# A third plane, -sin, in the rotation table of an S5 scan inside a two-block fp32 kernel

## The chip, the cores and the metric

The kernel runs on one core of one Trainium2 chip. The metric is device time in microseconds (us), median of several runs. A profiled execution of the kernel gives the rows shown below; their times count from the start of that execution's span. Engines are named as the profile names them: PE (matmuls) and PEld (its weight loads), DVE (VectorE), ACT (ScalarE), POOL (GpSimd), SP (SyncE, which here only issues DMAs).

## The reference, cut to what matters

Two blocks in sequence, all in fp32. Block 1 has two layers of four kinds of attention (differential, windowed, neighbourhood, query/key-normalised), each with an input projection, heads and an output projection. Block 2 has an input projection, a latent attention, a state-space branch (S5), a gated unit and a convolutional feed-forward network. Only the S5 branch computes what the change touches. For each of 32 groups of 128 complex states it runs, over the 272 time steps held (the last 258 are used),

```
x[t] = lambda * x[t-1] + B u[t]          (complex, one lambda per state)
y[t] = Re(C x[t]) + D u[t],   then a tanh-gelu
```

The kernel writes lambda as r * exp(i*theta) and rotates: with m[t] = exp(-i*theta*t) * (B u)[t], the scan g[t] = r * g[t-1] + m[t] has a real factor, so the real and the imaginary part are two separate real scans, and x[t] = exp(i*theta*t) * g[t]. The table of cos(theta*t) and sin(theta*t) for one group n is 2 planes of 128 x 272 values.

## The kernel before

**Weights.** All large matmuls are fp32 done as three passes over split operands: a weight tile of 128x1024 is loaded by SP into `raw` (3 buffers), ACT casts its high part `wh` (L314, 4 buffers), DVE subtracts to get the low part `wl` (L328), and PE runs 24 matmuls on the tile: data high x wh (L468), data low x wh (L469), data high x wl (L470). The method `take` asks for `wl` of the tile at hand and for `wh` of up to three tiles after it, so ACT's casts are issued, in program order, ahead of PE's use.

**Side work.** Other work is written as Python generators that are advanced a step at each `yield`, a few steps per weight tile, so its instructions stand between those of the tiles on each engine's queue. Every engine runs its queue strictly in the order of the program.

**The table.** `s5_tables` is such side work. It runs beside block 1's second layer, from about 1377 to 1777 us: first the input projection and heads (to about 1720 us), then the output projection (the "out phase", weight tiles 280 to 311, which ends at about 1771 us). For each n = 0..31 it copies 32 columns into a tile `et` (ACT, L1056), doubles the table in four levels, four DVE instructions each (L1068 to L1071; the last level is 16 wide, so the row `L1071 ... 128x16` is the last piece of an n), and stores the tile to the DRAM table `etab` by a DMA that POOL issues (L1072). `et` has two buffers. The 2 KB tiles that `t2k` hands out (`ea`, `eb`, `tb`, `bo`, the output phase's `sq`, the gate's `gt`) share a ring of three buffers with the tag `t2`.

**The out phase.** For every pair of output rows ACT copies the sums (`hb`, L1489) and squares them (`sq`, L1494), and POOL adds the squares up (`acc`, L1496). At its end PE sums over partitions (L577), POOL raises to -1/2 (`rr`, L584), PE transposes `rr`, and block 2 starts.

**The use.** `s5()` runs beside block 2's input projection and heads, from about 1827 to 2082 us. SP loads `e` (one n of `etab`, 2 buffers); `rotate` (L1812) makes two products on DVE, each over both planes (L1817), two sums of 272 (L1818, L1819), two scans (L1822), and on POOL two products of 516 (L1825) and two sums of 258 (L1826, L1827).

Of the kernel before, what the change touches and what calls it, by code (L numbers as in the profile page):

```python
# [11 lines left out]
F32 = mybir.dt.float32  # L12
F32R = mybir.dt.float32r
I32 = mybir.dt.int32
AF = mybir.ActivationFunctionType
ALU = mybir.AluOpType
AX = mybir.AxisListType
ADD, SUB, MUL, MAX = ALU.add, ALU.subtract, ALU.mult, ALU.max
# [79 lines left out]
NT = 272  # L98
NQ = 258
# [146 lines left out]
def program(ctx: ExitStack, tc: tile.TileContext, A, stop=None):  # L246
    nc = tc.nc
    V, S, P, T, SY = nc.vector, nc.scalar, nc.gpsimd, nc.tensor, nc.sync
# [4 lines left out]
    dram = ctx.enter_context(tc.tile_pool(name="dram", bufs=1, space=bass.MemoryType.DRAM))  # L253
# [286 lines left out]
    gpo = const.tile([128, 2, 16], F32, name="gpo")  # L540
    s5r = const.tile([128, 32], F32, name="s5r")
    acc272 = const.tile([128, NT], F32, name="acc272")
    etab = dram.tile([32, 128, 2, NT], F32, name="etab")

    btab = dram.tile([2, 32, 32, 2, 128], F32, name="btab")
    half = cst("half", [128, 2], "half")
# [67 lines left out]
    def t2k(name="t2"):  # L614
        return aw.tile([128, 512], F32, tag="t2", name=name, bufs=3)
# [295 lines left out]
    def s5_tables():  # L911
# [83 lines left out]
        for i in range(2):  # L995
            n0 = 16 * i
            b = aw.tile([128, 2, NT], F32, tag="mraw", name="bri", bufs=2).rearrange("p v t -> p (v t)")[:, :512]
            SY.dma_start(out=b, in_=A["bri"][:, n0:n0 + 16].rearrange("p n v c -> p (n v c)"))
            b = b.rearrange("p (n v c) -> p n v c", v=2, c=16)
            yield  # L1000
            yield
            fr, fi = (s5f[:, v, n0:n0 + 16].unsqueeze(2).to_broadcast([128, 16, 16]) for v in range(2))
            for v, op in enumerate((SUB, ADD)):
                tab = t2k("tb").rearrange("p (a n c) -> p a n c", a=2, c=16)
                V.tensor_tensor(out=tab[:, 0], in0=b[:, :, v, :], in1=fr, op=MUL)
                V.tensor_tensor(out=tab[:, 1], in0=b[:, :, 1 - v, :], in1=fi, op=MUL)
                V.tensor_tensor(out=tab[:, 0], in0=tab[:, 0], in1=tab[:, 1], op=op)
                o = t2k("bo").rearrange("p (n g c) -> p n g c", g=2, c=16)
                for g_ in range(2):
                    S.activation(out=o[:, :, g_, :], in_=tab[:, 0], func=AF.Copy, scale=half[:, g_:g_ + 1])  # L1010
                yield
                yield from hold()
                pt, of = ps_("X"), o.rearrange("p n g c -> p (n g c)")
                for q in range(4):
                    T.transpose(pt[:, 128 * q:128 * q + 128], of[:, 128 * q:128 * q + 128], ident)
                yield
                hl = [aw.tile([128, 512], F32R, tag="t2", name="bhl", bufs=3) for _ in range(2)]
                split(hl[0], hl[1], pt)
                lock["X"] = False
                for b_, t in zip(range(2), hl):  # L1020
                    P.dma_start(out=btab[b_, n0:n0 + 16, :, v, :].rearrange("(q a) c p -> (a c) q p", a=4), in_=t.bitcast(F32).rearrange("p (q s) -> p q s", q=4))
# [14 lines left out]
        for n in range(32):  # L1036
            e = aw.tile([128, 2, NT], F32, tag="mraw", name="et", bufs=2)
            if n % 8 == 0:
                V.memset(e0[:, :, 0, 0:1], 1.0)
                V.memset(e0[:, :, 1, 0:1], 0.0)  # L1040
                for lev in range(5):
                    if lev > 1:
                        yield
                        yield
                    tab = t2k("ea").rearrange("p (v n t) -> p v n t", v=2, n=8)
                    L = 1 << lev
                    c, s_ = (pw[:, lev, v, n:n + 8].unsqueeze(2).to_broadcast([128, 8, L]) for v in range(2))
                    xr, xi, er, ei = (e0[:, :, v, i * L:i * L + L] for i in range(2) for v in range(2))
                    ta, tb = tab[:, 0, :, :L], tab[:, 1, :, :L]
                    V.tensor_tensor(out=ta, in0=xi, in1=s_, op=MUL)  # L1050
                    V.tensor_tensor(out=tb, in0=xi, in1=c, op=MUL)
                    V.tensor_tensor(out=er, in0=xr, in1=c, op=MUL)
                    V.tensor_tensor(out=ei, in0=xr, in1=s_, op=MUL)
                    V.tensor_tensor(out=er, in0=er, in1=ta, op=SUB)
                    V.tensor_tensor(out=ei, in0=ei, in1=tb, op=ADD)
            S.copy(out=e[:, :, 0:32], in_=e0[:, n % 8])  # L1056
            for lev in range(5, 9):
                if lev < 8 and (lev != 6 or n % 2):
                    yield
                    yield  # L1060
                if lev < 8:
                    tab = t2k("eb").rearrange("p (v t) -> p v t", v=2)
                L = 1 << lev
                w = min(L, NT - L)
                c, s_ = pw[:, lev, 0, n:n + 1], pw[:, lev, 1, n:n + 1]
                er, ei = e[:, 0, L:L + w], e[:, 1, L:L + w]
                ta, tb = tab[:, 0, :w], tab[:, 1, :w]
                V.tensor_scalar(ta, e[:, 1, :w], s_, None, op0=MUL)  # L1068
                V.tensor_scalar(tb, e[:, 1, :w], c, None, op0=MUL)
                V.scalar_tensor_tensor(out=er, in0=e[:, 0, :w], scalar=c, in1=ta, op0=MUL, op1=SUB)  # L1070
                V.scalar_tensor_tensor(out=ei, in0=e[:, 0, :w], scalar=s_, in1=tb, op0=MUL, op1=ADD)  # L1071
            P.dma_start(out=etab[n], in_=e)  # L1072


    have, done_o = {}, {}
# [572 lines left out]
    def ring(tag, n, bufs):  # L1648
        return mw.tile([128, n], F32, tag=tag, name=tag, bufs=bufs)

    def chunks(t, off, n, w):
        return [t[:, off + i * w:off + i * w + w] for i in range(n)]
# [3 lines left out]
    ZF = zb(F32)  # L1656
# [131 lines left out]
    def s5():  # L1788
# [8 lines left out]
        def load_e(n):  # L1797
            c = mw.tile([128, 2, 32], F32, tag="ct", name="ct", bufs=7)
            SY.dma_start(out=c, in_=A["ct"][n])
            e = mw.tile([128, 2, NT], F32, tag="e", name="e", bufs=2)  # L1800
            SY.dma_start(out=e, in_=etab[n])
            return e, c

# [6 lines left out]
            return t  # L1810

        def rotate(n, bu, e):  # L1812
            co, si = e[:, 0, :], e[:, 1, :]
            m = ring("a1", 2 * NT, 1).rearrange("p (v t) -> p v t", v=2)
            g = ring("a2", 2 * NT, 2).rearrange("p (v t) -> p v t", v=2)
            for o, b in ((m, bu[0]), (g, bu[1])):
                V.tensor_tensor(out=o, in0=b[:, :NT].unsqueeze(1).to_broadcast([128, 2, NT]), in1=e, op=MUL)  # L1817
            V.tensor_tensor(out=m[:, 0, :], in0=m[:, 0, :], in1=g[:, 1, :], op=ADD)  # L1818
            V.tensor_tensor(out=m[:, 1, :], in0=m[:, 1, :], in1=g[:, 0, :], op=SUB)  # L1819
            rr = s5r[:, n:n + 1].to_broadcast([128, NT])  # L1820
            for v in range(2):
                V.tensor_tensor_scan(g[:, v, :], rr, m[:, v, :], 0.0, op0=MUL, op1=ADD)  # L1822
            o, o_ = (ring(t, 2 * NQ, k).rearrange("p (v t) -> p v t", v=2) for t, k in (("pr0", 5), ("pr", 1)))
            for x, w in ((o, co), (o_, si)):
                P.tensor_tensor(out=x, in0=g[:, :, 14:], in1=w[:, 14:].unsqueeze(1).to_broadcast([128, 2, NQ]), op=MUL)  # L1825
            P.tensor_tensor(out=o[:, 0, :], in0=o[:, 0, :], in1=o_[:, 1, :], op=ADD)  # L1826
            P.tensor_tensor(out=o[:, 1, :], in0=o[:, 1, :], in1=o_[:, 0, :], op=SUB)  # L1827
            out = [o[:, v, :] for v in range(2)]
            return out

        todo = deque()

        def gelu(j, yps):
            y, w = ring("gy", NQ, 1), ring("gw", NQ, 1)

            def a():
                V.scalar_tensor_tensor(out=y, in0=uF(j), scalar=dsk[:, j:j + 1], in1=yps[:, :NQ], op0=MUL, op1=ADD)
                S.activation(out=w, in_=y, func=AF.Square, scale=math.sqrt(0.044715))

            def b():  # L1840
                V.scalar_tensor_tensor(out=w, in0=w, scalar=1.0, in1=y, op0=ADD, op1=MUL)
                S.activation(out=w, in_=w, func=AF.Tanh, scale=math.sqrt(2 / math.pi))

            def c():
                V.scalar_tensor_tensor(out=w, in0=w, scalar=1.0, in1=y, op0=ADD, op1=MUL)
                S.activation(out=gF(j), in_=w, func=AF.Copy, scale=0.5)
                S.activation(out=uu[0][j][:, :NQ], in_=w, func=AF.Copy, scale=0.5)

            def d():
                V.tensor_tensor(out=uu[1][j][:, :NQ], in0=gF(j), in1=uu[0][j][:, :NQ].bitcast(F32), op=SUB)  # L1850

            todo.extend((a, b, c, d))
# [494 lines left out]
```

## Time and profile before

| what | value |
|---|---|
| median of 3 runs | 2967.01 us (2963.41 to 2968.47) |
| the profiled execution's own time | 2966.05 us |
| its span | 2964.0 us |
| PE busy | 2779.8 us, 94% |
| DVE busy | 1932.1 us, 65% |
| ACT busy | 1252.2 us, 42% |
| POOL busy | 489.5 us, 17% |

The span is what the profile's rows cover; the execution's own time is 2.05 us more. PE is busy for almost all of the span, and the other engines for a half or less on average. These averages cover stages that differ, so the rows below are taken from the stretches that the change touches.

### The profile page before, as it was taken

The page shows a single profiled execution, that of the slowest core. Times are in us where ns is not written, and L with a number is a line of the kernel's source. Part 1 is how long each engine was busy: PE and PEld are TensorE (multiplying, and loading weights), DVE is VectorE, ACT ScalarE, POOL GpSimd, SP SyncE. Part 2 cuts the span into 40 slices and gives each one's busy share as a digit, 9 for nine tenths or more (in the row PEclk, how much of TensorE's full clock was granted, in tenths as well). Part 3 has the DMA queues.
Part 4 walks back from the last instruction along what each step waited for, and adds up shares of the span by engine and source line. Part 5 has one row for each costly group of instructions (what it writes and reads, how often), then busy time and mean ns, then how long its engine had stood idle before and what let it go on. Part 6 is the DMA issues. An engine that isn't in the chain of part 4 may idle for free. (4 is left out here: it accounts for less than half of the span.)

```text
span 2964.0 us, 48919 instructions
## 1 busy us (share of the span) xinstructions
PE 2779.8 (94%) x18910; PEld 2503.3 (84%) x18910; DVE 1932.1 (65%) x3670; ACT 1252.2 (42%) x2169; POOL 489.5 (17%) x505
## 2 busy tenths in 40 slices
PE   5999999998999978999998999888999999999998
PEld 3778988886778968888998897655999999999998
DVE  4277777686777588756666784776665565456544
ACT  3445334243442445534445542134454444344443
POOL 0001000001111260100001124754231110011100
PEclk8999999999999989999999999987999999999999
DMA  9744445543346645534433464542555555555554
GB/s 366 269 143 135 132 153 156 160 140 121 121 135 192 223 155 197 166 101 135 151 126 112 138 200 154 170 140 69 158 161 182 184 184 182 186 185 183 184 178 150
DMA packets 183817, 487.31 MB, mean 164 GB/s; under 512 B 28064, under 2 KB 39968, under 8 KB 183584
## 3 DMA queue, kind: packets, MB, share of 16 engines
q1 hardware_dynamic: 178368, 470.93, 50.1%
q0 software_dynamic: 3200, 11.01, 1.1%
q8 instruction: 148, 2.42, 0.3%
q10 hardware_dynamic: 2016, 2.25, 0.2%
q14 instruction: 85, 0.70, 0.1%
HBM read 467.66 MB, written 13.11 MB: 162 GB/s over the span
## 5 line engine op out<-in xcount | busy, mean ns | idle before, releaser
L328 DVE TENSOR_TENSOR wl<-raw,wh 128x1024 fp32r<-128x1024 f32 x620 | 765.4, 1239 | 437.9 <-ACT wh L314 437.1
L314 ACT CAST wh<-raw 128x1024 fp32r<-128x1024 f32 x620 | 639.4, 1036 | 861.1 <-PE mm L469 548.4
L468 PE MATMUL mm<-nH,wh 128*128 128x256 f32 (+1 forms) x2016 | 694.8, 345 | 9.8 <-ACT kp L1143 6.7
L469 PE MATMUL mm<-nL,wh 128*128 128x256 f32 (+1 forms) x2016 | 687.7, 341 | 4.7 <-DVE nL L1131 4.7
L470 PE MATMUL mm<-nH,wl 128*128 128x256 f32 (+1 forms) x2016 | 687.0, 341 | 3.8 <-DVE wl L328 3.7
L468 PEld LDWEIGHTS mm<-nH,wh 128*128 128x128 f32 x2016 | 386.6, 192 | 59.6 <-ACT kp L1143 7.1
L470 PEld LDWEIGHTS mm<-nH,wl 128*128 128x128 f32 x2016 | 386.1, 192 | 50.4 <-DVE wl L328 4.8
L469 PEld LDWEIGHTS mm<-nL,wh 128*128 128x128 f32 x2016 | 386.5, 192 | 49.8 <-DVE nL L1131 6.5
L468 PE MATMUL mm<-ZA,wh 128*128 128x258 f32 (+1 forms) x1408 | 400.1, 284 | 5.0 <-DVE oa L1923 5.0
L470 PE MATMUL mm<-ZA,wl 128*128 128x258 f32 (+1 forms) x1408 | 399.5, 284 | 0.0
L469 PE MATMUL mm<-ZB,wh 128*128 128x258 f32 (+1 forms) x1290 | 363.5, 282 | 0.0
L693 DVE SCALAR_TENSOR_TENSOR acc<-mraw,cs,acc 128x512 f32<-128x512 f32 x420 | 296.3, 756 | 46.0 <-DMA mraw<-in_wmod 44.5
L468 PEld LDWEIGHTS mm<-ZA,wh 128*128 128x128 f32 x1408 | 267.0, 190 | 5.3 <-issue 5.2
L470 PEld LDWEIGHTS mm<-ZA,wl 128*128 128x128 f32 x1408 | 267.1, 190 | 0.0
L469 PEld LDWEIGHTS mm<-ZB,wh 128*128 128x128 f32 x1290 | 245.0, 190 | 0.0
L374 PE MATMUL mm<-wh,nH 128*128 128x256 f32 x736 | 212.9, 289 | 3.5 <-ACT nH L1567 3.5
L376 PE MATMUL mm<-wh,nL 128*128 128x256 f32 x736 | 211.2, 287 | 1.6 <-DVE nL L1569 1.5
L375 PE MATMUL mm<-wl,nH 128*128 128x256 f32 x736 | 210.5, 286 | 0.0
L468 PE MATMUL mm<-yH,wh 128*128 128x256 f32 x688 | 193.3, 281 | 0.0
L469 PE MATMUL mm<-yL,wh 128*128 128x256 f32 x688 | 193.3, 281 | 0.0
L470 PE MATMUL mm<-yH,wl 128*128 128x256 f32 x688 | 193.3, 281 | 0.0
L2285 POOL TENSOR_TENSOR v<-v,a 128x256 f32<-128x256 f32 x43 | 59.4, 1382 | 562.8 <-ACT a L2284 549.6
(497 smaller groups left out, 4644.1 us busy)
## 6 DMA issues: line engine op xcount, KB each, us to landing
raw<-in_win SPq DMA_DIRECT2D x266, 512.0 KB, 3.8
raw<-in_wup SPq DMA_DIRECT2D x172, 512.0 KB, 4.3
mraw<-in_wmod SPq DMA_DIRECT2D x256, 256.0 KB, 2.8
raw<-in_wout SPq DMA_DIRECT2D x76, 512.0 KB, 3.8
raw<-in_wda SPq DMA_DIRECT2D x40, 512.0 KB, 3.5
raw<-in_wdb SPq DMA_DIRECT2D x40, 512.0 KB, 4.2
mraw<-in_wmodf SPq DMA_DIRECT2D x30, 512.0 KB, 8.4
mraw<-in_wmodf SPq DMA_DIRECT2D x9, 1024.0 KB, 10.3
```

Source lines behind the costliest of these rows:

```text
L314: S.copy(out=h[:, :size], in_=self.raw[j][:, :size])
L328: V.tensor_sub(lo[:, :size], r[:, :size], h[:, :size].bitcast(F32))
L374: T.matmul(o, ah, w[i][0], start=(k == 0 and t % 2 == 0), stop=False)
L375: T.matmul(o, ah, w[i][1], start=False, stop=False)
L376: T.matmul(o, al, w[i][0], start=False, stop=(k == nk - 1 and t % 2 == 1 and last and i == len(w) - 1))
L468: T.matmul(out, wh, ah, start=start, stop=False)
L469: T.matmul(out, wh, al, start=False, stop=False)
L470: T.matmul(out, wl, ah, start=False, stop=stop)
L693: V.scalar_tensor_tensor(out=acc, in0=w, scalar=cs[:, k, v:v + 1], in1=acc, op0=MUL, op1=ADD)
L2285: P.tensor_tensor(out=v, in0=v, in1=a, op=MUL)
```

## The change

The table gets a third plane. For each n, ACT makes -sin from the finished tile (`neg`, a `t2` tile), and a second DMA from POOL's queue stores it, so that `etab[n]` holds -sin, cos, sin. In `rotate` the first factor is multiplied by planes 1 and 2 (cos, sin) and the second by planes 0 and 1 (-sin, cos), the sign of the imaginary part being turned in the table of B, so that both parts of the result come from one sum of 544 on DVE and, after the scans, one sum of 516 on POOL. POOL's two products now read one scan's result each. The load of `e` is of three planes. For the sign, one `tensor_tensor` in the making of the B table becomes a `scalar_tensor_tensor`. `gelu` takes two pieces of a free buffer for y and w in place of ring tiles.

```diff
--- before.py
+++ after.py
@@ -540,7 +540,8 @@
     gpo = const.tile([128, 2, 16], F32, name="gpo")
     s5r = const.tile([128, 32], F32, name="s5r")
     acc272 = const.tile([128, NT], F32, name="acc272")
-    etab = dram.tile([32, 128, 2, NT], F32, name="etab")
+
+    etab = dram.tile([32, 128, 3, NT], F32, name="etab")
 
     btab = dram.tile([2, 32, 32, 2, 128], F32, name="btab")
     half = cst("half", [128, 2], "half")
@@ -1000,11 +1001,15 @@
             yield
             yield
             fr, fi = (s5f[:, v, n0:n0 + 16].unsqueeze(2).to_broadcast([128, 16, 16]) for v in range(2))
-            for v, op in enumerate((SUB, ADD)):
+            for v in range(2):
                 tab = t2k("tb").rearrange("p (a n c) -> p a n c", a=2, c=16)
                 V.tensor_tensor(out=tab[:, 0], in0=b[:, :, v, :], in1=fr, op=MUL)
                 V.tensor_tensor(out=tab[:, 1], in0=b[:, :, 1 - v, :], in1=fi, op=MUL)
-                V.tensor_tensor(out=tab[:, 0], in0=tab[:, 0], in1=tab[:, 1], op=op)
+                if v:
+
+                    V.scalar_tensor_tensor(out=tab[:, 0], in0=tab[:, 0], scalar=-1.0, in1=tab[:, 1], op0=MUL, op1=SUB)
+                else:
+                    V.tensor_tensor(out=tab[:, 0], in0=tab[:, 0], in1=tab[:, 1], op=SUB)
                 o = t2k("bo").rearrange("p (n g c) -> p n g c", g=2, c=16)
                 for g_ in range(2):
                     S.activation(out=o[:, :, g_, :], in_=tab[:, 0], func=AF.Copy, scale=half[:, g_:g_ + 1])
@@ -1069,7 +1074,10 @@
                 V.tensor_scalar(tb, e[:, 1, :w], c, None, op0=MUL)
                 V.scalar_tensor_tensor(out=er, in0=e[:, 0, :w], scalar=c, in1=ta, op0=MUL, op1=SUB)
                 V.scalar_tensor_tensor(out=ei, in0=e[:, 0, :w], scalar=s_, in1=tb, op0=MUL, op1=ADD)
-            P.dma_start(out=etab[n], in_=e)
+            neg = t2k("neg")[:, :NT]
+            S.activation(out=neg, in_=e[:, 1, :], func=AF.Copy, scale=-1.0)
+            P.dma_start(out=etab[n][:, 1:3], in_=e)
+            P.dma_start(out=etab[n][:, 0], in_=neg)
 
 
     have, done_o = {}, {}
@@ -1797,7 +1805,7 @@
         def load_e(n):
             c = mw.tile([128, 2, 32], F32, tag="ct", name="ct", bufs=7)
             SY.dma_start(out=c, in_=A["ct"][n])
-            e = mw.tile([128, 2, NT], F32, tag="e", name="e", bufs=2)
+            e = mw.tile([128, 3, NT], F32, tag="e", name="e", bufs=2)
             SY.dma_start(out=e, in_=etab[n])
             return e, c
 
@@ -1810,28 +1818,25 @@
             return t
 
         def rotate(n, bu, e):
-            co, si = e[:, 0, :], e[:, 1, :]
+
             m = ring("a1", 2 * NT, 1).rearrange("p (v t) -> p v t", v=2)
             g = ring("a2", 2 * NT, 2).rearrange("p (v t) -> p v t", v=2)
-            for o, b in ((m, bu[0]), (g, bu[1])):
-                V.tensor_tensor(out=o, in0=b[:, :NT].unsqueeze(1).to_broadcast([128, 2, NT]), in1=e, op=MUL)
-            V.tensor_tensor(out=m[:, 0, :], in0=m[:, 0, :], in1=g[:, 1, :], op=ADD)
-            V.tensor_tensor(out=m[:, 1, :], in0=m[:, 1, :], in1=g[:, 0, :], op=SUB)
+            for o, b, w in ((m, bu[0], e[:, 1:3]), (g, bu[1], e[:, 0:2])):
+                V.tensor_tensor(out=o, in0=b[:, :NT].unsqueeze(1).to_broadcast([128, 2, NT]), in1=w, op=MUL)
+            V.tensor_tensor(out=m, in0=m, in1=g, op=ADD)
             rr = s5r[:, n:n + 1].to_broadcast([128, NT])
             for v in range(2):
                 V.tensor_tensor_scan(g[:, v, :], rr, m[:, v, :], 0.0, op0=MUL, op1=ADD)
             o, o_ = (ring(t, 2 * NQ, k).rearrange("p (v t) -> p v t", v=2) for t, k in (("pr0", 5), ("pr", 1)))
-            for x, w in ((o, co), (o_, si)):
-                P.tensor_tensor(out=x, in0=g[:, :, 14:], in1=w[:, 14:].unsqueeze(1).to_broadcast([128, 2, NQ]), op=MUL)
-            P.tensor_tensor(out=o[:, 0, :], in0=o[:, 0, :], in1=o_[:, 1, :], op=ADD)
-            P.tensor_tensor(out=o[:, 1, :], in0=o[:, 1, :], in1=o_[:, 0, :], op=SUB)
-            out = [o[:, v, :] for v in range(2)]
-            return out
+            for x, v in ((o, 0), (o_, 1)):
+                P.tensor_tensor(out=x, in0=g[:, v, 14:].unsqueeze(1).to_broadcast([128, 2, NQ]), in1=e[:, v:v + 2, 14:], op=MUL)
+            P.tensor_tensor(out=o, in0=o, in1=o_, op=ADD)
+            return o[:, 1, :], o[:, 0, :]
 
         todo = deque()
 
         def gelu(j, yps):
-            y, w = ring("gy", NQ, 1), ring("gw", NQ, 1)
+            y, w = chunks(ZF, 2576, 2, NQ)
 
             def a():
                 V.scalar_tensor_tensor(out=y, in0=uF(j), scalar=dsk[:, j:j + 1], in1=yps[:, :NQ], op0=MUL, op1=ADD)
```

On ACT, at the out phase's tiles with n = 24, 25, the rows before (`et` copy L1056, casts `wh`, `hb` and `sq` of the output rows):

```order
L314 CAST wh<-raw 128x1024 [waits DMAHW1_49,PE_49,Activation_49]
L1056 COPY et<-scr 128x2x32 [waits DMASW7_49]
L314 CAST wh<-raw 128x1024 [waits DMAHW2_49,PE_49,Activation_49]
L1489 COPY hb<-mm 128x256 [waits PE_49]
L1494 ACTIVATE sq<-mm 128x256 [waits DVE_49,Pool_49]
L1489 COPY hb<-mm 128x256
L1494 ACTIVATE sq<-mm 128x256 [waits DVE_49]
L314 CAST wh<-raw 128x1024 [waits DMAHW3_49,Activation_49]
L1056 COPY et<-scr 128x2x32 [waits DMASW0_49,Activation_49]
L314 CAST wh<-raw 128x1024 [waits DMAHW4_49,PE_49,Activation_49]
```

and the same place after the change (`neg` is L1078, the copies `et` are L1061, `hb` L1497, `sq` L1502):

```order
L314 CAST wh<-raw 128x1024 [waits DMAHW1_49,PE_49]
L1078 ACTIVATE neg<-et 128x272 [waits DMASW5_49,DVE_49,Activation_49]
L1061 COPY et<-scr 128x2x32 [waits DMASW6_49]
L314 CAST wh<-raw 128x1024 [waits DMAHW2_49,PE_49]
L1497 COPY hb<-mm 128x256 [waits PE_49]
L1502 ACTIVATE sq<-mm 128x256 [waits DVE_49,Pool_49]
L1497 COPY hb<-mm 128x256
L1502 ACTIVATE sq<-mm 128x256 [waits DMASW1_49,Activation_49]
L314 CAST wh<-raw 128x1024 [waits DMAHW3_49]
L1078 ACTIVATE neg<-et 128x272 [waits DVE_49,Activation_49]
L1061 COPY et<-scr 128x2x32 [waits DMASW0_49]
L314 CAST wh<-raw 128x1024 [waits DMAHW4_49,PE_49]
```

`neg` of an n stands directly ahead of the copy that opens the next n, with a wait for DVE; the second `sq` of the pair now waits for a DMA of POOL's queue (DMASW) where it waited for DVE.

On POOL, one n of `rotate` (`pr` with a number is the first product's tile, `a` with a number the scans' result), before:

```order
L1825 TENSOR_TENSOR pr_18395<-a_18388,e 128x516 [waits DMAHW7_49,DVE_49]
L1825 TENSOR_TENSOR pr<-a_18388,e 128x516
L1826 TENSOR_TENSOR pr_18395<-pr_18395,pr 128x258 [waits Pool_49]
L1827 TENSOR_TENSOR pr_18395<-pr_18395,pr 128x258
L1749 TENSOR_TENSOR acc<-acc,sq 128x258 [waits Activation_49]
```

and after:

```order
L1832 TENSOR_TENSOR pr_18490<-a_18484,e 128x516 [waits DMAHW7_49,DVE_49]
L1832 TENSOR_TENSOR pr<-a_18484,e 128x516 [waits DVE_49]
L1833 TENSOR_TENSOR pr_18490<-pr_18490,pr 128x516 [waits Pool_49]
L1757 TENSOR_TENSOR acc<-acc,sq 128x258 [waits Activation_49]
```

Two sums have become one of twice the width, and each product has a wait for DVE of its own. PE's queue has the same instructions in the same order in both kernels.

## Rows read from the trace of the kernel before

**Rows 1.** Two windows: length; busy us (count) of PE, PEld, DVE, ACT, POOL; clock, DMA.

```profile
1720.00:1760.00 40.00, 38.79 (x321) 38.02 (x320) 38.21 (x131) 18.69 (x32) 9.14 (x12) 1.00 0.64 204
1820.00:2100.00 280.00, 233.88 (x1103) 171.31 (x1103) 199.34 (x385) 78.27 (x226) 150.91 (x155) 0.86 0.43 132
```

**Rows 2.** Timeline of ACT in the out phase: start, length, instruction, [idle before].

```profile
1736.10 0.24 ACT L1056 COPY et<-scr 128x64 f32<-128x64 f32 x1
...
1741.32 0.39 ACT L1494 ACTIVATE sq<-mm 128x256 f32<-128x256 f32 x1
1741.60 1.04 ACT L314 CAST wh<-raw 128x1024 fp32r<-128x1024 f32 x1
1743.94 0.24 ACT L1056 COPY et<-scr 128x64 f32<-128x64 f32 x1 [1.30 <-DMA etab<-et]
```

**Rows 3.** Timeline of DVE in the same stretch.

```profile
1740.44 0.23 DVE L1071 SCALAR_TENSOR_TENSOR et<-et,pw,eb 128x16 f32<-128x16 f32 x1
...
1741.20 1.22 DVE L328 TENSOR_TENSOR wl<-raw,wh 128x1024 fp32r<-128x1024 f32 x1
...
1744.04 1.22 DVE L328 TENSOR_TENSOR wl<-raw,wh 128x1024 fp32r<-128x1024 f32 x1
...
1746.66 1.21 DVE L328 TENSOR_TENSOR wl<-raw,wh 128x1024 fp32r<-128x1024 f32 x1
```

**Rows 4.** Timeline of PE: its first use of the first of these wl tiles.

```profile
1742.47 0.39 PE L470 MATMUL mm<-nH,wl 128*128 128x256 f32 x1
```

**Rows 5.** POOL's store of a table tile: one in the timeline, and landing of all 32.

```profile
1741.47 0.56 POOL L1072 DMA_DIRECT2D etab<-et  x1 [10.55 <-ACT hb L1489]
...
DMA to landing us min/median/max: 2.3/2.7/4.4
```

**Rows 6.** Timelines of DVE, ACT and PE about the end of n = 14.

```profile
1600.63 0.24 ACT L1056 COPY et<-scr 128x64 f32<-128x64 f32 x1
...
1602.79 0.23 DVE L1071 SCALAR_TENSOR_TENSOR et<-et,pw,eb 128x16 f32<-128x16 f32 x1
...
1603.73 0.42 ACT L1197 ACTIVATE sqa<-kp 128x256 f32<-128x256 f32 x1
...
1604.20 0.49 PE L557 MATMUL X<-ones,sqa 128*128 128x1 f32 x3 [2.05 <-ACT sqa L1197]
```

**Rows 7.** Timelines of ACT, DVE and PE about the end of n = 17.

```profile
1682.10 1.02 ACT L1129 CAST nH<-hb 128x256 fp32r<-128x256 f32 x3
...
1685.86 0.23 DVE L1071 SCALAR_TENSOR_TENSOR et<-et,pw,eb 128x16 f32<-128x16 f32 x1
...
1686.47 0.38 PE L469 MATMUL mm<-nL,wh 128*128 128x256 f32 x1 [1.02 <-DVE nL L1131]
```

**Rows 8.** Timelines of ACT, DVE, PE and POOL where the out phase ends.

```profile
1767.80 0.24 ACT L1056 COPY et<-scr 128x64 f32<-128x64 f32 x1 [2.22 <-DMA etab<-et]
...
1769.45 0.23 DVE L1071 SCALAR_TENSOR_TENSOR et<-et,pw,eb 128x16 f32<-128x16 f32 x1
1769.60 0.23 DVE L1068 TENSOR_SCALAR eb<-et,pw 128x32 f32<-128x32 f32 x1
...
1774.24 0.56 PE L577 MATMUL PT<-ones,acc 128*128 128x1 f32 x2 [3.13 <-ACT hb L1489]
...
1777.01 0.54 POOL L1072 DMA_DIRECT2D etab<-et  x1 [3.12 <-issue]
1777.57 0.73 POOL L584 TENSOR_TENSOR rr<-rv,mhalf 128x2 f32<-128x2 f32 x1
```

**Rows 9.** The rotation's lines: count, ns min/median/max, first and last start.

```profile
L1817 DVE TENSOR_TENSOR a<-bu,e x64: 701/715/726, 1827.8 to 2071.4; 128x544 f32<-128x544 f32 x64
...
L1818 DVE TENSOR_TENSOR a<-a,a x32: 441/444/1391, 1829.1 to 2072.1; 128x272 f32<-128x272 f32 x32
...
L1822 DVE TENSOR_TENSOR_SCAN a<-s5r,a x64: 692/724/1178, 1830.0 to 2073.6; 128x272 f32<-128x272 f32 x64
...
L1825 POOL TENSOR_TENSOR pr<-a,e x64: 1267/1284/2287, 1831.4 to 2075.7; 128x516 f32<-128x516 f32 x64
```

## The prediction

> **What bounds the kernel now.** I began with the page's totals: PE is busy 94% of the span, so time moves where PE waits. The change touches two stretches, and I took the windows of both next. In the out phase, where the table is still being made, DVE is as full as PE, 38.21 and 38.79 of 40 us, and ACT has 18.69 [rows 1]. There the weight stream is a chain ACT (wh), DVE (wl), PE, and the timelines show how tight it is: the wl that starts at 1741.20 ends at 1742.42 [rows 3], and PE takes it at 1742.47 [rows 4]. What DVE loses here, PE loses 0.05 us later, and DVE has 1.8 us free in 40 to make it good. In the S5 stretch PE is busy 233.88 of 280 us, DVE 199.34, POOL 150.91 [rows 1]: room on all of them, with rotations that begin 7.86 us apart ((2071.4 - 1827.8) / 31 from the first to the last L1817) [rows 9]. Last I read, on ACT's queue, where the new instruction stands, since ACT's total says nothing on its order.
>
> **The place of neg.** neg(n) stands in ACT's queue directly ahead of the copy that opens the next n, and needs the last DVE piece of its own n. Before, ACT reached that place early: copy(25) ran at 1736.10 [rows 2], and the last piece of n = 24 at 1740.44 to 1740.67 [rows 3]. The copy never needed that piece; neg does. So ACT, which has time to spare but no way round, stands still for up to 4.6 us, and everything queued behind it is late: wh casts, hb, sq, nH. The waits of which that is true and someone needs the late thing are my sum. neg itself I price at 0.42 us, from an activation of 256 columns on ACT [rows 6]; it has 272.
>
> **n = 24, 26, 28 (out phase).** neg from 1740.67, then the copy (0.24) and the next cast (1.04, both in rows 2): 1740.67 + 0.42 + 0.24 + 1.04 = 1742.37, so the wl of 1741.20 starts some 1.2 late. Then a second wait: neg takes one of the three t2 tiles, and its DMA holds the tile until it has landed; the second sq of the pair gets this tile. The store of e was issued at 1741.47 for 0.56 us [rows 5], the store of neg stands behind it: 1742.03, and a landing takes 2.7 [rows 5], so sq runs at 1744.75 in place of 1741.32 [rows 2], the cast behind it at 1745.03 (sq and cast stand 0.28 apart in rows 2) to 1746.07, and its wl at 1746.07 in place of 1744.04 [rows 3]. That is 2.03 in all, the first 1.2 within it.
>
> **n = 25, 27.** No sq here. The wl of 1746.66 stood right behind the last piece of n = 25 [rows 3], with its cast made long before. Now neg, copy and cast lie between: 0.42 + 0.24 + 1.04 = 1.70. For the five: 3 x 2.03 + 2 x 1.70 = 9.5. DVE's free 1.8 of 40 us is no cover, since it comes from the same waits; I take nothing off.
>
> **n = 14.** ACT passed the place at 1600.63 and did 3.1 us of work and short waits before the sqa at 1603.73 on which PE waited 2.05 us [rows 6]. Now neg waits for 1602.79 + 0.23 = 1603.02, and the copy follows 0.4 later. With some 0.3 of those waits absorbed, sqa comes at 1603.4 + 2.8 = 1606.2 or a little earlier: 2.3 late, and PE with it.
>
> **n = 16, 17.** The casts nH of 1682.10, then long done, now come behind neg(17), which waits until 1686.09 [rows 7]. neg and copy 0.66, the first of three casts 0.34: nL can start at 1687.1 and no longer at the end of the last piece, 1686.0, where PE was already waiting for it [rows 7]: 1.0. For n = 16 the same sequence stands there, and I give it the same. n = 18 and 22 I allow 0.4 each, a choice, since there the late casts are partly of tiles ahead. At the other n the wh buffers, up to three tiles ahead, cover it, at nothing; without that cover each would cost the 1.7 of n = 25.
>
> **The end of the out phase.** No tile is left to hide anything: PE waits 3.13 us for hb, which comes behind the copies [rows 8]. copy(30) ran at 1767.80; neg(29) waits until 1769.68, so copy(30) ends at 1769.68 + 0.42 + 0.24 = 1770.34 and the piece of n = 30 that began at 1769.60 [rows 8] is 0.7 late. neg(30) stands before copy(31), 0.4 more. And POOL raised rr directly after the last store, which it issued in 0.54 us [rows 8]; the store of neg(31) now stands between: 0.55. Sum 1.65.
>
> **S5: the sums.** Two sums at 0.444 become one; 544 columns take 0.715 on DVE (L1817) [rows 9]. That is 0.17 of DVE a rotation, 5.5 us over 32, of which a part would reach PE, which waits for several things there. POOL's fused sum of 516 I price as its product of 516, 1.284 [rows 9], the same as two halves of it. But DVE and POOL block each other: L1818 takes 441 to 1391 ns, and L1825 1267 to 2287, while L1817, one input of which comes from PSUM, stays at 701 to 726 [rows 9]. A rule speaks against the change here: the Trainium skill, "SBUF — State Buffer", section "Who interferes with whom", says that a VectorE instruction with two inputs in SBUF and a GpSimd instruction that reads SBUF take turns, whoever began holding the ports for its whole length. The rows agree. By that rule POOL's sum holds DVE off for 1.28 in one piece and not in two, and an instruction that comes at random inside waits 0.64 on average and not 0.32; with four such instructions of DVE a rotation of 7.86 us, that is 4 x (1.28/7.86) x 0.32 = 0.2, an estimate, or 6.7 us of DVE lost over 32, where without the rule nothing is lost.
>
> Without either sentence the bounds are the same two: at best the 5.5 us reach the end, at worst each of 32 sums meets a block of the length that the rows show once (1.391 - 0.441 = 0.95) a quarter of the time, 7.6. With PE idle in 46 of 280 us I let half of either through: -3 to +4, and take 0. The new load of e is 408 KB in place of 272 KB: at 132 GB/s for 0.43 of the queues' time [rows 1], 307 GB/s when busy, that is 0.44 us more a rotation; hidden under the 7.86 by the second buffer of e, 14 us if it were not. gelu's tiles and the sign in B's table keep their counts and widths: nothing.
>
> **Sum.** 9.5 + 2.3 + 2.0 + 0.8 + 1.65 = 16.3. The profiled execution took 2966.05 us by its own time, 0.96 under the median, so 2966.05 + 16.3 = 2982.3, and 1 more for the median: I say 2983.
>
> **The rivals.**
> *The buffers hide it.* ACT has 21 us free in 40 [rows 1], and a wh is cast up to three tiles ahead. For it: wh of the wl at 1744.04 was ready at 1742.64 [rows 2, 3], a margin of 1.4. Against it: the delay of that cast is 3.4. If the margin were 3.4 everywhere, what is left would be the end of the out phase and half of n = 14: 2967 + 1.65 + 1.15 = 2970; if those are hidden too, 2967.
> *Faster: S5 gives more than the table costs.* POOL's first product needs only the first of two scans, which may let it begin a scan, 0.72 [rows 9], earlier, and DVE saves its 5.5 us. If PE's 46 idle us of S5 fall by a fifth, 9 us, and the table is hidden as above: 2959. It decides from the point at which the waits for neg cost under 9. Against it: the second scan also reads two tiles in SBUF and would be running by then, so that by the blocking in the rows POOL's product starts behind it anyway.
> *The clock falls as well.* The granted clock is 1.00 (2.4 GHz) in the out phase, where PE idles 1.2 of 40 us, and 0.86 on average in S5, where it idles 46 of 280 [rows 1]. With 10 us of new idle time in 50 the out phase could look like S5: 50 x (1/0.86 - 1) = 8 more, 2991.
>
> **Chances.** Forecast (2975 to 2988) 0.67; clock 0.18, up to 2994; hidden 0.10, both of its times within the bound below, but for a chance of 0.01; faster 0.05. About 0.2%, 6 us, is what a measurement of this kernel can tell from no change. A slower result: 0.67 + 0.18 + 0.01 for a hidden case that leaves more = 0.86; same 0.09; faster 0.05. The range, 2971 to 2993, leaves out the hidden and the faster case and the end of the clock's.
>
> **What the next profile would show.** ACT: before each copy of et a wait for DVE's et, and in the out phase before the second sq a wait for a DMA of POOL. DVE: in 1720 to 1760 idle time before wl, 4 to 8 us in 40, with ACT's wh as releaser, and PE's idle time before L470 likewise. PE's wait before L557 grows from 2.05 to over 4. The end of the out phase, PE's L577, comes some 15 us later than 1774.24, and from there to the end of S5 the distance is the same within 4. I am wrong if wl keeps its place although ACT waits; if PE's waits in S5 fall by more than 5 us; or if neg takes much more than 0.42.

## The result, and the profile after

The changed kernel took 2993.90 us (median, 2992.83 to 2997.49), the kernel before 2966.28 beside it: a ratio of 1.0096, 95% interval 1.0083 to 1.0108, or 27.6 us slower. The direction was right and the size was not: 16 us were forecast, and the time lies 0.9 us above the upper end of the range. (One execution of the experiment that gives neg a tile of its own was slow, 4473.16 us at a granted clock of 0.556 where the others had 0.963 to 0.965, and is left out of that run's figures.)

The page of the changed kernel, its totals:

```profile
PE 2787.9 (93%) x18910; PEld 2505.0 (84%) x18910; DVE 1937.2 (65%) x3638; ACT 1261.5 (42%) x2201; POOL 516.9 (17%) x505
```

DVE has 32 instructions fewer and 5 us more to do (it is busy for 65% of the span in both kernels, which is more than the "half or less" said above of the engines beside PE); no total says where 27 us went. PE's queue is the same in both kernels, so each of its instructions can be laid on its twin, and the difference of their starts says how late PE is at each place. (The changed trace starts 0.2 late.)

```
place in the kernel before             late   grown by
1420 (table begun)                      0.2
1440 (n = 1)                            2.7     2.5
1595 (n = 13)                           4.1     1.4
1610 (n = 14)                           7.6     3.5
1660 (a slow clock of before, gone)     5.2    -2.4
1720 (n = 16, 17, 18)                   7.1     1.9
1741 (n = 20 to 23, out phase)         10.0     2.9
1768 (n = 24 to 28)                    18.2     8.2
1770 (n = 29)                          19.3     1.1
1800 (end of the out phase)            21.6     2.3
2085 (end of S5)                       27.2     5.6
```

So 21.4 us were lost while the table is made, and 5.6 in S5. Of the first, 14.5 lie in the out phase and at its end. The window of the out phase in the kernel before and in the changed one (length, then busy us and count of PE, PEld, DVE, ACT, POOL, then clock and DMA):

```profile
1720.00:1771.00 51.00, 49.79 (x412) 48.83 (x410) 48.97 (x169) 22.28 (x40) 12.25 (x16) 1.00 0.65 210
```

```profile
1727.00:1790.00 63.00, 53.19 (x411) 49.51 (x410) 47.25 (x163) 26.07 (x51) 16.79 (x25) 1.00 0.60 189
```

and the waits in it (us in total, times, longest), first one line of before, then the change:

```profile
DVE wl L328 <- ACT wh L314: 3.7, 2, 2.4
```

```profile
DVE wl L328 <- ACT wh L314: 13.6, 11, 3.0
ACT neg L1078 <- DVE et L1076: 11.8, 3, 4.5
...
PE mm L470 <- DVE wl L328: 7.5, 11, 1.0
...
ACT sq L1502 <- DMA etab<-neg: 6.7, 4, 2.3
...
PE mm L468 <- ACT wh L314: 2.2, 4, 1.5
```

PE takes 63 us for what took 51 before, DVE has fallen from 48.97 busy us in 51 to 47.25 in 63, and the chain is there link by link: neg waits for DVE's last piece, the casts stand behind neg, DVE's wl waits for the cast, PE for wl. ACT's and DVE's timelines about n = 24, which answer to [rows 2] and [rows 3]:

```profile
1750.74 0.43 ACT L1078 ACTIVATE neg<-et 128x272 f32<-128x272 f32 x1 [4.53 <-issue]
...
1751.22 1.04 ACT L314 CAST wh<-raw 128x1024 fp32r<-128x1024 f32 x1
...
1754.26 0.39 ACT L1502 ACTIVATE sq<-mm 128x256 f32<-128x256 f32 x1 [1.19 <-DMA etab<-neg]
1754.54 1.04 ACT L314 CAST wh<-raw 128x1024 fp32r<-128x1024 f32 x1
```

```profile
1750.43 0.23 DVE L1076 SCALAR_TENSOR_TENSOR et<-et,pw,eb 128x16 f32<-128x16 f32 x1
...
1752.29 1.23 DVE L328 TENSOR_TENSOR wl<-raw,wh 128x1024 fp32r<-128x1024 f32 x1 [0.24 <-ACT wh L314]
...
1755.61 1.23 DVE L328 TENSOR_TENSOR wl<-raw,wh 128x1024 fp32r<-128x1024 f32 x1 [0.91 <-ACT wh L314]
...
1759.97 1.23 DVE L328 TENSOR_TENSOR wl<-raw,wh 128x1024 fp32r<-128x1024 f32 x1 [1.64 <-ACT wh L314]
```

ACT stands idle for 4.53 us ("issue" means that the profile found no releaser here) and starts neg at 1750.74, right behind the piece of 1750.43, which ends at 1750.66. Both later waits are there: sq for the store of neg, then the cast and the wl behind it.

At n = 14 and at the end of the out phase, against [rows 6] and [rows 8] (the second fence is PE's row for rr in the kernel before):

```profile
1610.60 1.02 PE L558 MATMUL X<-ones,sqa 128*128 128x1 f32 x4 [4.25 <-ACT sqa L1205]
...
1795.68 0.56 PE L578 MATMUL PT<-ones,acc 128*128 128x1 f32 x2 [5.26 <-ACT hb L1497]
...
1797.38 0.99 PE L578 MATMUL PT<-ones,sq 128*128 128x1 f32 x4
1800.51 1.22 PE L589 MATMUL PT<-ident,rr 128*128 128x128 f32 x4 [2.14 <-POOL rr L585]
...
1798.46 0.43 ACT L1078 ACTIVATE neg<-et 128x272 f32<-128x272 f32 x1 [2.87 <-PE PT L578]
...
1799.18 0.54 POOL L1080 DMA_DIRECT2D etab<-neg  x1 [1.36 <-ACT neg L1078]
1799.73 0.72 POOL L585 TENSOR_TENSOR rr<-rv,mhalf 128x2 f32<-128x2 f32 x1
```

```profile
1778.36 1.22 PE L588 MATMUL PT<-ident,rr 128*128 128x128 f32 x4 [1.43 <-POOL rr L584]
```

PE's wait before its L557 (now L558) has grown from 2.05 to 4.25, that for hb from 3.13 to 5.26, that for rr from 1.43 to 2.14, and rr stands behind the store of neg(31), which came late because neg(31) waited for PE's L578: that reads the last squares, in tiles of the t2 ring.

In S5, the lines of the rotation and, below them, four instructions of gelu on DVE, each with two tensors as inputs (count, ns min/median/max). One of the four stands directly behind the scans in 23 of the 32 rotations. The first, L1842, reads one of its tensors from PSUM; the other three read both from SBUF, and in 16 rotations it is one of these three.

```profile
L1826 DVE TENSOR_TENSOR a<-a,a x32: 724/726/1783, 1850.7 to 2099.3; 128x544 f32<-128x544 f32 x32
...
L1832 POOL TENSOR_TENSOR pr<-a,e x64: 1263/1468/1613, 1852.3 to 2102.4; 128x516 f32<-128x516 f32 x64
...
L1833 POOL TENSOR_TENSOR pr<-pr,pr x32: 1268/1277/2160, 1855.2 to 2104.0; 128x516 f32<-128x516 f32 x32
...
L1842 DVE SCALAR_TENSOR_TENSOR ZB<-hb,dsk,y x8: 452/457/483, 1883.1 to 2113.3; 128x258 f32<-128x258 f32 x8
...
L1846 DVE SCALAR_TENSOR_TENSOR ZB<-ZB x8: 969/1439/1467, 1889.3 to 2114.7; 128x258 f32<-128x258 f32 x8
...
L1850 DVE SCALAR_TENSOR_TENSOR ZB<-ZB x8: 412/626/1437, 1891.3 to 2116.7; 128x258 f32<-128x258 f32 x8
...
L1855 DVE TENSOR_TENSOR ZA<-hb,ZA x8: 976/1434/1460, 1896.7 to 2122.8; 128x258 fp32r<-128x258 f32 x8
```

The first and the last of those three in the kernel before:

```profile
L1841 DVE SCALAR_TENSOR_TENSOR gw<-gw,gy x8: 395/402/970, 1868.5 to 2087.5; 128x258 f32<-128x258 f32 x8
...
L1850 DVE TENSOR_TENSOR ZA<-hb,ZA x8: 397/402/974, 1876.9 to 2095.3; 128x258 fp32r<-128x258 f32 x8
```

The fused sums cost what was forecast, 0.726 and 1.277. But POOL's product, unchanged in width, went from a median of 1.284 [rows 9] to 1.468, and two of gelu's instructions from 0.40 to 1.43. One of them in DVE's and POOL's timelines, after the change and, below, at the same place before:

```profile
1957.58 1.34 DVE L1829 TENSOR_TENSOR_SCAN a<-s5r,a 128x272 f32<-128x272 f32 x2
1958.84 1.43 DVE L1855 TENSOR_TENSOR ZA<-hb,ZA 128x258 fp32r<-128x258 f32 x1
...
1958.44 2.97 POOL L1832 TENSOR_TENSOR pr<-a,e 128x516 f32<-128x516 f32 x2 [3.21 <-PE y L1873]
```

```profile
1935.67 1.34 DVE L1822 TENSOR_TENSOR_SCAN a<-s5r,a 128x272 f32<-128x272 f32 x2
1936.92 0.40 DVE L1850 TENSOR_TENSOR ZA<-hb,ZA 128x258 fp32r<-128x258 f32 x1
...
1937.14 2.57 POOL L1825 TENSOR_TENSOR pr<-a,e 128x516 f32<-128x516 f32 x2 [2.50 <-PE y L1868]
```

POOL begins within the second scan and is at work when DVE comes to gelu; the first of its two products takes 1.55 of the 2.97 us and ends at 1959.99, and gelu's instruction at 1960.27. It is the same in all 16 rotations in which an instruction with both inputs in SBUF stands there: it takes 1.43 to 1.47 us. L1842 at that place keeps its 0.46. In the kernel before, POOL began behind both scans, 0.2 us after gelu's instruction, which kept its 0.40.

### The profile page after: what moved, and what is told of

Its sections match the earlier page's. It is cut to its first block, busy times and chain, and to the rows that moved or that the text cites. A ratio compares the mean times of both kernels' runs of the same rounds, so it can differ in the third digit from the quotient of the medians.

```text
span 2991.0 us, 49000 instructions
## 1 busy us (share of the span) xinstructions
PE 2787.9 (93%) x18910; PEld 2505.0 (84%) x18910; DVE 1937.2 (65%) x3638; ACT 1261.5 (42%) x2201; POOL 516.9 (17%) x505
```

## The experiments

Ratios are to the kernel before on the same chip, in brackets their 95% intervals. The runs were made on several chips, so they are compared by their ratios. "S5" is how much longer the stretch from 1800 to 2085 of before is in that trace.

**No negation.** The place of neg, or the second store and the larger tables?

```diff
-            neg = t2k("neg")[:, :NT]
-            S.activation(out=neg, in_=e[:, 1, :], func=AF.Copy, scale=-1.0)
             P.dma_start(out=etab[n][:, 1:3], in_=e)
-            P.dma_start(out=etab[n][:, 0], in_=neg)
+            P.dma_start(out=etab[n][:, 0], in_=e[:, 1, :])
```

> Leaves out the negation: no neg on ACT, and the second store takes plane sin from the tile itself, so plane 0 holds sin in place of -sin; the two stores, the larger load and the fused sums stay. Theory 1 (ACT stands still at neg, and what is queued behind it is late): of the 27.6 us nearly all of the 21.6 that PE has lost by the end of the table's making goes, but for POOL's second store before rr, 0.6; the loss in S5, 5.6, stays: about 2973 us. Theory 2 (the second store on POOL's queue and the larger tables cost it): nothing changes, 2990 or more.

1.0041 (1.0028 to 1.0053), 2975.62 us; PE was 3.5 late at 1800 in place of 21.6, S5 +3.5. Nearly all of the loss of the table's making goes with the negation on ACT. This trace was 0.6 late when the table began, so 2.9 of 21.4 us stay. Of these, 1.6 lie at n = 20 to 23, where ACT's copy of et waits longer for the tile's stores (5.58 us against 4.68 before): here the second store reads that tile too, which it does not in the change.

**The table alone, in the kernel before.** neg and both stores as in the change, load and rotation as before. (`etab` has three planes in this run and the next one too; `...` marks lines left out of a diff.)

```diff
-            P.dma_start(out=etab[n], in_=e)
+            neg = t2k("neg")[:, :NT]
+            S.activation(out=neg, in_=e[:, 1, :], func=AF.Copy, scale=-1.0)
+            P.dma_start(out=etab[n][:, 1:3], in_=e)
+            P.dma_start(out=etab[n][:, 0], in_=neg)
...
-            SY.dma_start(out=e, in_=etab[n])
+            SY.dma_start(out=e, in_=etab[n][:, 1:3])
```

> The kernel before with the third plane made and stored (neg on ACT, two stores), while the load and the rotation are those of before. Theory 1: the loss up to the end of the table's making, 21.6 us, and nothing in S5: 2988 us. If the S5 loss came from the table too (a later or other start of the stretch): 2993.

1.0079 (1.0066 to 1.0092), 2986.13 us; late by 20.3 at 1800, S5 -0.5. The two halves of the loss are separate.

**Two stores in the kernel before, without a negation.**

```diff
-            P.dma_start(out=etab[n], in_=e)
+            P.dma_start(out=etab[n][:, 1:3], in_=e)
+            P.dma_start(out=etab[n][:, 0], in_=e[:, 1, :])
...
-            SY.dma_start(out=e, in_=etab[n])
+            SY.dma_start(out=e, in_=etab[n][:, 1:3])
```

> The kernel before with a second store of plane sin for each n (no negation, no ACT work), and load and rotation as before. Against the run without a negation it differs by the change in S5 alone (fused sums and the load of three planes). If the second store costs what PE lost by the end of the table's making in that run, 3.5: 2970. If S5's part is the 3.6 that the same trace shows, this run is 3.6 us under that one; if S5's part is nothing, they agree within their intervals.

1.0011 (1.0001 to 1.0022), 2968.95 us, late by 2.1 at 1800. By the ratios it is 0.0030, some 9 us, under the run without a negation (6.7 by the medians), and the intervals do not overlap, so S5's change costs some us by the times too. But this trace's S5, which is that of before, came out at +3.2 with more time at the lower clock. One trace of S5 is good to about 3 us.

**A tile of its own for neg.**

```diff
-            neg = t2k("neg")[:, :NT]
+            neg = aw.tile([128, NT], F32, tag="neg", name="neg", bufs=1)
```

> After the change, with a tile of its own for neg in place of one of the three t2 tiles, so that no sq waits for a store to land; neg keeps its place on ACT and its wait for DVE. Prediction's first term (second sq's wait, 2.03 in place of 1.2, at n = 24, 26, 28): 2.5 us less, 2991. If the place of neg alone costs the time: 2994. If the t2 tiles are most of it: 2980 or less.

1.0093 (1.0079 to 1.0108), 2991.24 us: not told apart from the change by its time. In the trace no sq waits for a store, wl waits for wh 8.2 us in the out phase and not 13.6, and the out phase grew by 8.5 and not by 12.2, so the second wait is real and three tenths of it in the trace; the rest stays with neg in its place.

**neg on POOL.**

```diff
-            neg = t2k("neg")[:, :NT]
-            S.activation(out=neg, in_=e[:, 1, :], func=AF.Copy, scale=-1.0)
+            neg = aw.tile([128, NT], F32, tag="neg", name="neg", bufs=1)
             P.dma_start(out=etab[n][:, 1:3], in_=e)
+            P.tensor_scalar(neg, e[:, 1, :], -1.0, None, op0=MUL)
             P.dma_start(out=etab[n][:, 0], in_=neg)
```

> After the change, with neg made by POOL between its two stores, in a tile of its own; ACT does nothing new. Theory 1: ACT's waits are gone, and the time is that of the run without a negation, about 10 us over before (2976), with 1 more for the longer POOL queue ahead of rr. Rival: POOL's reading of SBUF, 32 times some 0.7 us, blocks DVE's two-input instructions, which in the out phase are as full as PE: 9 times up to 0.7, 5 us more, 2982.

1.0051 (1.0037 to 1.0064), 2977.61 us. The instruction took 0.903 us at the median on POOL, twice ACT's, and the out phase grew by 3.2. ACT's waits for neg are gone, as theory 1 says. The 5 us that the rival expected from a blocked DVE did not show in the out phase's length: without any negation it grew by 2.7.

**neg late.** The same ACT instruction, issued in the middle of the next n, ahead of its third level.

```diff
+        pend = []
...
+                if lev == 7 and pend:
+                    pend.pop()()
...
-            neg = t2k("neg")[:, :NT]
-            S.activation(out=neg, in_=e[:, 1, :], func=AF.Copy, scale=-1.0)
             P.dma_start(out=etab[n][:, 1:3], in_=e)
-            P.dma_start(out=etab[n][:, 0], in_=neg)
+
+            def put(n=n, e=e):
+                neg = aw.tile([128, NT], F32, tag="neg", name="neg", bufs=1)
+                S.activation(out=neg, in_=e[:, 1, :], func=AF.Copy, scale=-1.0)
+                P.dma_start(out=etab[n][:, 0], in_=neg)
+            pend.append(put)
+        pend.pop()()
```

> After the change, with neg of an n and its store issued in the middle of the next n's levels, when the last DVE piece of its n has long been done, in a tile of its own; ACT does the same 32 instructions of 0.43 us. Theory 1 (it is the wait at that place, not the work): about 10 us over before, 2976. If ACT's added work itself costs: 32 x 0.43 = 14 more, 2990.

1.0029 (1.0018 to 1.0040), 2972.07 us. Its window of the out phase and two of its waits:

```profile
1725.00:1776.00 51.00, 50.11 (x412) 48.92 (x411) 49.03 (x169) 24.81 (x47) 16.70 (x23) 1.00 0.73 228
...
DVE wl L328 <- ACT wh L314: 4.0, 2, 2.7
...
PE mm L470 <- DVE wl L328: 0.8, 3, 0.4
```

ACT does 32 negations as before, and the out phase is 51 us again. It was the wait at that place, not the work. (This trace is 4.4 late before the table begins, and 5.3 at 1800.) S5: +5.8.

**POOL's products swapped**, so that the first needs the second scan again.

```diff
-            for x, v in ((o, 0), (o_, 1)):
+            for x, v in ((o_, 1), (o, 0)):
```

> POOL's two products of a rotation in the other order, so that the first one needs the second scan, as before the change. Theory C (POOL's product now starts within the second scan, holds the ports for 1.55 us and makes DVE's two-input instruction behind the scans wait, 0.4 to 1.43 us): the 5.6 us of S5 go and the saving of DVE's fused sum (0.3 a rotation) shows in part: 2985 us, give or take 3. Theory D (the product is dearer in its new form, 1.47 in place of 1.28 us, whatever it meets): L1832 stays at 1.47 and the time at 2994.

1.0093 (1.0079 to 1.0107), 2991.58 us: no clear gain over the change's 1.0096. S5 was +2.9, and the mean of L1832 1.338, of L1846 0.471 us, as before the change; but PE was 23.0 late at 1800, 1.4 more than in the change. So theory C's 2985 did not come, though its instructions changed as it says. Theory D, that the product is dearer in its new form, is out: the form is the same here.

**POOL's half as before**, DVE's fused sum and the load of three planes kept.

```diff
-            for x, v in ((o, 0), (o_, 1)):
-                P.tensor_tensor(out=x, in0=g[:, v, 14:].unsqueeze(1).to_broadcast([128, 2, NQ]), in1=e[:, v:v + 2, 14:], op=MUL)
-            P.tensor_tensor(out=o, in0=o, in1=o_, op=ADD)
-            return o[:, 1, :], o[:, 0, :]
+            for x, w in ((o, e[:, 1]), (o_, e[:, 2])):
+                P.tensor_tensor(out=x, in0=g[:, :, 14:], in1=w[:, 14:].unsqueeze(1).to_broadcast([128, 2, NQ]), op=MUL)
+            P.tensor_tensor(out=o[:, 0, :], in0=o[:, 0, :], in1=o_[:, 1, :], op=ADD)
+            P.tensor_tensor(out=o[:, 1, :], in0=o[:, 1, :], in1=o_[:, 0, :], op=SUB)
+            return o[:, 0, :], o[:, 1, :]
```

> After the change, with POOL's half of the rotation as before (two products over both scans, two sums of 258); DVE's fused sum, the load of three planes and the table stay. Theory C: as with the swap, about 2985 us, since POOL starts behind the scans again. If it is DVE's fused sum or the larger load that costs the 5.6: 2994.

1.0086 (1.0072 to 1.0099), 2990.14 us, S5 +2.2. Theory C's 2985 us would be 1.0071, just outside the interval; the 1.0079 of the table alone and the 1.0096 of the change both lie within it. With the table's waits still there, neither run settles S5; so the next four were made on the late neg, where the table costs nothing.

**Late neg with the swap.** The diffs of the late neg and of the swap together.

> The late neg, and POOL's two products in the other order (the first needs the second scan). The late neg alone ran at 1.0029 of before, of which S5 5.8 us by its trace. Theory C (POOL's earlier start makes DVE's instruction behind the scans wait): L1857 and its like fall from 1.4 to some 0.4 us, and 3 to 5 us go: 1.0015. If the earlier start does no harm on the path: 1.0029 as with the late neg alone.

0.9997 (0.9986 to 1.0009), 2965.19 us, S5 -1.3: more went than the 3 to 5 us that theory C expected. The lines that answer to L1846, L1850 and L1855 of the change:

```profile
L1853 DVE SCALAR_TENSOR_TENSOR ZB<-ZB x8: 395/400/967, 1870.6 to 2088.2; 128x258 f32<-128x258 f32 x8
...
L1857 DVE SCALAR_TENSOR_TENSOR ZB<-ZB x8: 394/416/940, 1871.4 to 2090.2; 128x258 f32<-128x258 f32 x8
...
L1862 DVE TENSOR_TENSOR ZA<-hb,ZA x8: 398/401/974, 1878.1 to 2096.5; 128x258 fp32r<-128x258 f32 x8
```

**Late neg with POOL's half as before.**

> The late neg, and POOL's half of the rotation as before; DVE's fused sum and the load of three planes stay. Theory C: 1.0010 or under, the S5 stretch within 2 of before's 290 us. If the fused sum of DVE or the larger load costs the S5 loss: 1.0029.

0.9998 (0.9985 to 1.0010), 2965.35 us, S5 +2.8: the time is theory C's, the stretch a little over its 2. This run and the one above keep DVE's fused sum, the larger load and gelu's new tiles, so none of these costs the S5 loss by itself.

**Late neg with load and rotation as before.**

> The late neg and its store, with load and rotation as before: the table alone, without the wait. Theory 1: the table is hidden, but for POOL's store before rr: 1.0000 to 1.0010. If the table has a cost of its own beside the wait: as the late neg alone, 1.0029.

1.0000 (0.9991 to 1.0008), 2965.96 us, S5 +0.6.

**Late neg with DVE's sums as before**, POOL's half as changed.

```diff
-            for o, b, w in ((m, bu[0], e[:, 1:3]), (g, bu[1], e[:, 0:2])):
-                V.tensor_tensor(out=o, in0=b[:, :NT].unsqueeze(1).to_broadcast([128, 2, NT]), in1=w, op=MUL)
-            V.tensor_tensor(out=m, in0=m, in1=g, op=ADD)
+            for o, b in ((m, bu[0]), (g, bu[1])):
+                V.tensor_tensor(out=o, in0=b[:, :NT].unsqueeze(1).to_broadcast([128, 2, NT]), in1=e[:, 1:3], op=MUL)
+            V.tensor_tensor(out=m[:, 0, :], in0=m[:, 0, :], in1=g[:, 1, :], op=SUB)
+            V.tensor_tensor(out=m[:, 1, :], in0=m[:, 1, :], in1=g[:, 0, :], op=ADD)
```

> The late neg, DVE's sums as before (two of 272), POOL's half as changed. Theory C: the S5 loss stays or grows, since POOL still starts within the second scan: 1.0029 or over, S5 295 us or over. If DVE's fused sum caused the loss: 1.0010.

1.0014 (1.0005 to 1.0023), 2969.75 us, S5 +6.5; its line for L1846:

```profile
L1854 DVE SCALAR_TENSOR_TENSOR ZB<-ZB x8: 970/1442/1444, 1868.5 to 2094.6; 128x258 f32<-128x258 f32 x8
```

The line and the stretch are those of theory C. The time is not: it lies between the two theories' 1.0010 and 1.0029, and its interval holds the first and not the second. That DVE's fused sum adds to the loss when POOL starts early is therefore not ruled out. Over all traces, the six in which POOL may start behind the first scan (the change, no negation, own tile, neg on POOL, late neg, and this one) have S5 at +3.5 to +6.5, mean 5.6; the seven others at -1.3 to +3.2, mean 1.4. The two groups do not overlap, but only 0.3 us lies between them; it is the means that can be told apart.

## Why the prediction was right or wrong

**Right: the place of neg.** That it waits for the last piece of its n, with casts and sq behind it, is what the trace shows and what the late neg takes away: the same instruction, some rows further down, costs nothing (1.0000 with the rest as before). The price of neg, forecast at 0.42, was 0.43. n = 24 to 28, forecast at 9.5, came to 8.2; n = 14, forecast at 2.3, to a wait longer by 2.2.

**Wrong in size: "at the other n the wh buffers cover it, at nothing".** In the out phase n = 20 to 23 cost 2.9 and n = 29 cost 1.1, where 0.4 for n = 22 was all that was allowed. So a cast up to three tiles ahead was no cover in a stretch where DVE is full: what one neg held up was not made good before the next. At n = 20 to 23 this is not the only way to lose time: the two runs with a second store from et and no negation lost 1.6 and 2.7 there; the late neg lost nothing. n = 13 cost some 1. n = 16 to 18, forecast at 2.4, cost 1.9 with 1.1 given back in between (see the clock), so some 3.0. The end of the out phase cost 2.3 and not 1.65. PE's wait for hb grew by 2.1, where 0.7 and 0.4 were forecast. Its wait for rr grew by 0.7: I had priced the length of the last store only, 0.55, and not that neg(31) would wait for a t2 tile that PE was reading; POOL stood still for 1.36 us ahead of that store. Some 0.5 was made good behind these two. In all, the table's making came to 21.4 where 16.3 was forecast, and with the 5.6 of S5 the time left the range by 0.9.

**The step that failed: S5 "take 0", bounds -3 to +4.** It came to 5.6, outside the bounds, and the sign "the same within 4" failed with it. One trace of S5 is good to about 3 us, but three pairs of runs that differ in the S5 part alone agree by their ratios: the change and the table alone (1.0096, 1.0079), no negation and two stores (1.0041, 1.0011), the late neg and the late neg with load and rotation as before (1.0029, 1.0000): 5 to 9 us. For the first pair the intervals overlap, for the other two they do not. The sum priced what the fused sums would meet; that POOL's products move stood only in the rival "faster", and two things there were wrong. I wrote that POOL's first product "starts behind" the second scan anyway; it starts within it (1958.44, the scans ending at 1958.92), so an earlier start was real. And I took an earlier start for a gain. What it changes is who waits: POOL's product of 1.55 us is now under way when DVE comes to gelu's instruction, and DVE loses 1.03 of the 1.43 us, in 16 of 32 rotations, some 16 us of DVE's time. Before, DVE was first by 0.2 us and lost nothing. The Trainium skill, "SBUF — State Buffer", section "Who interferes with whom", has the sentence "Issue order, not op shape, decides who blocks."; the traces agree (0.40 and 1.43 us for the same instruction), and I weighed that page for a random meeting of the two only, where the meeting is fixed by the program: half of the rotations have one such instruction at the same place. DVE's busy time in S5 rose by 8 us though its sums fell by 10 (20.8 + 20.1 to 31.1). That the order of POOL's two products decides it is shown by the swap on the late neg: 1.0029 to 0.9997, and the instructions back at 0.40. That it is all of the loss is not shown: with the table's waits in place the same swap brought no clear gain (1.0096, 1.0093), and with DVE's sums unfused and POOL still early the time was 1.0014.

**Clock.** The rival that the clock falls in the out phase did not come: 1.00 in the window above with PE idle for 10 of 63 us. Elsewhere the lower level (0.5, or 1.2 GHz) went both ways. At n = 14, where PE waits 4.25 us in place of 2.05, it lasted 6.83 us and not 3.41; beside the wait longer by 2.2, that step lost 1.3 more. Two stretches of it that the kernel before has, at 1650 to 1657 and at 1674 to 1678, are absent, which gave 2.6 and 1.1 back. At n = 1, PE lost 1.0 by a load of a bias table, for which DVE waited 4.07 us in place of 3.4, and 1.5 in 3.41 us at the lower level behind it; neg(1) ran only at 1431.15, when most of this was lost. The other traces with neg at that place on a t2 tile lost 0.8 to 2.8 there, those without it 0.0 to 0.8; what share the negation has in the 2.5 stays open. That these losses and gains nearly cancel is luck: none of them was in the sum.

**Also open:** why the late neg with all of the S5 saving (the swap) is no faster than before, 0.9997. DVE's fused sums save it time, and PE's S5 stretch does not shrink measurably: that other engines end PE's waits there is likely, but no run shows it. Nor was it followed, wait by wait, how DVE's 8 us became PE's 5.6.

## What to carry to other kernels

An instruction on an engine with time to spare is not free where it stands: ask what it waits for, whether the queue used to be past that place before the event, and what is behind it; moving it down to where its input is long done made it free here. When a dependence is loosened so that one engine may start earlier, ask which engine used to be first at what they share and will now be second: an earlier start on an engine off the path can be a loss. And a forecast that says "covered" for many repeats should be made for each of them in the stretch where the engines are full.

## What the runs showed of the hardware that was not expected

A POOL product that started within a DVE scan overlapped it by 0.48 us and took 1.55 us in place of 1.27; the scan kept its length (a median of 0.724 us in both kernels). Whether the product waited for a part of that overlap is open. The DVE instruction with both inputs in SBUF that came next ended 0.28 us behind the product, 1.43 us after its own start; one with an input in PSUM at the same place kept its 0.46. Negating 272 columns took 0.43 us on ACT and 0.90 us on POOL.
